# Another column order for the second token tile in every tail, and first products by arrival, in an encoder trunk

## The chip, the cores and the metric

The kernel runs on one core of one Trainium2 chip. The metric is the device time of one execution in microseconds, as the median of several executions. The kernel before took 935.35 us (median of three; 934.53 to 939.41). The profile shows one further execution.

## The reference

Two encoder layers of three sublayers each work on 256 tokens with 1024 features in fp32. So there are six stages: ffn, mLSTM, ffn, ffn, windowed attention, ffn. Each adds its result to a scaled x and normalises. Cut to what matters here:

```python
def swiglu(x, w_in, w_out):                       # w_in 1024 x 5632, w_out 2816 x 1024
    gu = x @ w_in
    g, u = gu[..., :D_FF], gu[..., D_FF:]
    return (jax.nn.silu(g) * u) @ w_out

for l in range(DEPTH):                            # DEPTH = 2
    x = layer_norm(ALPHA * x + 0.5 * swiglu(x, ffn_w_in[l, 0], ffn_w_out[l, 0]), ...)
    y = mlstm_mixer(x, ...) if l % 2 == 0 else window_attention(x, ...)
    x = layer_norm(ALPHA * x + y, ...)
    x = layer_norm(ALPHA * x + 0.5 * swiglu(x, ffn_w_in[l, 1], ffn_w_out[l, 1]), ...)
```

The mLSTM mixer projects x to q, k, v, output gate and 16 small gates (`gw` in the kernel), runs a chunked recurrence in both directions and projects back. Attention projects to q, k, v, attends within 128 tokens with a sink logit per head (`sink`), and projects back.

## The kernel before

**Products.** Every fp32 product is made of three single-pass products. Each operand is cut into a high part in TensorE's reduced fp32 form (ScalarE, `xT_hi`, `w_hi`, `h_hi`) and the rest (VectorE, `xT_lo`, `w_lo`, `h_lo`). `mm3` (L474) adds high by high, high by low and low by high into one PSUM bank. The stationary operand is a block of x or h transposed, 128 x 128; the moving one is 512 columns of a weight. The rows of the profile print them the other way: `pw<-w_hi,xT_lo` is the product of w's high and xT's low part. There are four PSUM banks named `pw` and four named `py`.

**Tokens and columns.** The 256 tokens are two tiles of 128, t = 0 and 1. A stage's output has 1024 columns, in two halves o = 0 and 1 of 512, so that y[t][o] takes the four `py` banks.

**Weights.** A piece is 128 x 1024 values. Its transfer (L102, issued by SyncE's queue) lands in one of four raw buffers (`w_raw`; six more, `s_raw`, hold pieces that are first added to one another, on VectorE or by an accumulating transfer that POOL issues, L265). `Weights.high` (L212) puts the split of ScalarE into the program, `Weights.low` (L236) that of VectorE. Both write into a ring of ten rooms. `Weights.take` (L288) hands pieces to the products; `Weights.done(upto, most)` (L297) says that the pieces before `upto` have had their last product, which opens rooms, and puts the splits of at most `most` further pieces into the program at this place. Within the ffn groups `Weights.fill` (L268) decides that instead, by a running model of the engines' times (`Paced`, L50). Transfers of raw pieces are issued, in the order of the plan, as the last reader of a raw buffer is done.

**Order.** The scheduler is switched off: every engine works through its instructions in the order in which the program wrote them, and waits at each until its operands are there. Because a helper records them, nearly all rows carry the line L136.

**The ffn.** One stage goes through its hidden columns in groups. `seven` (L727) takes a Strassen-like scheme with sums of x blocks (`S_hi`, `S_lo`) and of raw weights (`s_raw`). In the last group's `end4` VectorE multiplies by the activated gate (`e<-g,e`), and the block is transposed and split into `h_hi` and `h_lo` behind it.

**The tail.** `tail` (L554) ends a stage with the products of the last pieces: six in the ffn stages, eight in mLSTM, and in attention eight for tile 1. It runs over t, over o, and over the pieces. After each half `norm[t].half` adds the result to x (`x<-x,py`) and gathers its statistics; after both, `finish` (L533) makes rs with a power on POOL (L538) and normalises x in two passes, `x<-x,mv,ln_g` and `x<-x,rs,ln_b` (in two cuts each where `LC` says so). `emit_x(0)`, the transposes of tile 0's new x for the next stage, stands inside the last column pass of tile 1, at the piece `turn_at` = 4. The transposes of tile 1, `emit_x(1)`, are *pending*: the next stage runs them behind its first products, at the k-step that `PEND` gives. `TD` bounds how many splits stand behind the tail.

**The start.** While the first weights arrive, TensorE makes idle products on the identity (`warm`), transposes the first half of each token tile of x, and begins with the product of the first pieces.

**Small loads.** `small_loads` (L462) puts gate weights, gate biases and sinks on POOL's queue, with two negations; only mLSTM and attention use them.

Of the kernel before, what the change touches and what calls it, by code (L numbers as in the profile page):

```python
# [23 lines left out]
GROUPS = 3  # L24
# [7 lines left out]
FB = [1, 0, 1, 3, 2, 1, 0, 0, 1, 1, 0]  # L32
CT = [0, 1]
EX = [0, 1, 2, 2, 2, 2, 1, 2]
LC = [1, 0, 0, 0, 0, 1]
TD = [0, 3, 2, 0, 2, 1]
MP = [1, 0, 0, 0, 1, 0, 1, 1, 0, 0, 0, 0, 2, 2, 2]
PD = [8, 0, 7, 8, 5]
PEND = [6, 2, 6, 6, 6]


AHEAD = 300.0
# [276 lines left out]
def trunk_kernel(ctx: ExitStack, tc: tile.TileContext, x, ffn_w_in, ffn_w_out, ln_g, ln_b, ml_w_in, ml_gate_b,  # L319
                 ml_norm_g, ml_w_out, at_w_in, at_sink, at_w_out, out):  # L320
    nc = Paced(tc.nc)
# [152 lines left out]
    def mm3(o, l, r, start, stop, onto=False):  # L474
        nc.tensor.matmul(o, l[0], r[0], start=start, stop=False, skip_group_check=onto)
        nc.tensor.matmul(o, l[0], r[1], start=False, stop=False, skip_group_check=onto)
        nc.tensor.matmul(o, l[1], r[0], start=False, stop=stop, skip_group_check=onto)

    def pair(p, *idx):
        return p[0][idx], p[1][idx]  # L480
# [7 lines left out]
    A = slice(None)  # L488

    def tok(t):  # L490
        return slice(t * 128, (t + 1) * 128)

    def split_evac(dst, src, scale=None):
        if scale is None:
            nc.scalar.copy(dst[0], src)
            nc.vector.tensor_sub(dst[1], src, dst[0].bitcast(F32))
        else:
            nc.scalar.activation(dst[0], src, AF.Copy, scale=scale)
            nc.vector.scalar_tensor_tensor(dst[1], src, scale, dst[0].bitcast(F32), op0=OP.mult, op1=OP.subtract)

    def to_xT(t, src, bank, halves=range(2)):
        for h in halves:
            p = bank((128, 4, 128))
            for k in range(4):
                nc.tensor.transpose(p[:, k], src[:, (4 * h + k) * 128:(4 * h + k + 1) * 128], ident)
            split_evac(pair(xT, A, slice(4 * h, 4 * h + 4), tok(t)), p)

    def warm(n):

# [43 lines left out]

    def tail(y, h, todo, first, norm, last, turn_at, between=None):  # L554

        for t in range(2):
            for o in range(2):
                final = t == 1 and o == 1
                for n, (c, (i, w)) in enumerate(todo[t]):
                    if between is not None and t == 0 and o == 1 and n == turn_at:  # L560
                        between()
                    if final and n == turn_at:
                        emit_x(0, last)
                    mm3(y[t][o], h(c, t), pair(w, A, 0, slice(o * 512, o * 512 + 512)),
                        first and n == 0, n == len(todo[t]) - 1)
                    if final and n >= turn_at - 1:
                        W.done(i + 1, (0, 3, 0)[min(n - turn_at + 1, 2)])
                norm[t].half(o, y[t][o])
            norm[t].finish(t)
        W.done(most=TD[bound[0]])  # L570
        return lambda: emit_x(1, last)

    def emit_x(t, last):
        if not last:
            to_xT(t, xt[t], ybank)

    def ffn(l, i, n, pending, last):
        with ExitStack() as ph:
# [10 lines left out]
            start = pending is None  # L589
            if start:  # L590
                warm(14)
                to_xT(0, xt[0], ybank, (0,))
                W.split(1)
                warm(8)
                to_xT(1, xt[1], ybank, (0,))
                W.split(2)
            hs, pieces = [], []

            def tr(hB, t, h):
# [10 lines left out]
            def b_mm(ps, t, m, a):  # L610
                if 4 * m + a == len(pieces):
                    pieces.extend(W.take(1))
                for k in (2 * a, 2 * a + 1):
                    mm3(ps, pair(xT, A, k, tok(t)), pair(pieces[4 * m + a], A, k % 2), k == 0, k == 7)

            def b_silu(ps):
                sg = temp("sg")
# [38 lines left out]
            if start:  # L656
                sg = {}
                for m in range(2):
                    ps = [wbank(), wbank()]
                    for a in range(4):  # L660
                        if m == 0 and a == 1:
                            for t in range(2):
                                to_xT(t, xt[t], ybank, (1,))
                        for t in range(2):
                            b_mm(ps[t], t, m, a)
                            if m == 1 and a == 3:
                                b_mul(sg[t], ps[t])
                        early = {2: lambda: x_raw(0), 3: lambda: x_raw(1), 4: x_one, 5: x_two, 6: x_rest}
                        if 4 * m + a in early:
                            early[4 * m + a]()  # L670
                        W.done()
                    if m == 0:
                        W.open(pool, ends[bound[0]])
                        for t in range(2):
                            sg[t] = b_silu(ps[t])
            else:
                W.open(pool, ends[bound[0]])
                for t in range(2):
                    ps = [wbank(), wbank()]
                    for m in range(2):  # L680
                        for a in range(4):
                            if t == 0 and m == 1 and 2 * a == PEND[bound[0] - 1]:
                                pending()
                            b_mm(ps[m], t, m, a)
                            if t == 1:
                                W.done(W.used - 8 + 4 * m + a + 1)
                            if t == 1 and a % 2:
                                [[None, lambda: x_raw(0), None, lambda: x_raw(1)], [None, x_one, None, lambda: None]][m][a]()
                        if m == 0:
                            sg = b_silu(ps[0])  # L690
                            if t == 1:
                                tr(hB, 0, hs[0])
                    b_mul(sg, ps[1])
                x_two()
                W.done()
# [17 lines left out]
            def product(bank, x_of, first, then):  # L713

                for j in range(2):
                    w, = W.take(1)
                    for k in range(2):
                        mm3(bank, x_of(2 * j + k), pair(w, A, k), first and j == k == 0, j == k == 1, not first)
                then()
                W.done()  # L720
# [6 lines left out]
            def seven(full, unit_turn):  # L727

                of = lambda k0, t: (lambda k: pair(xT, A, k0 + k, tok(t)))
                sum_ = lambda name: (lambda k: pair(xs[name], A, k))  # L730
                v = {}
                hB = h_room(4)
                chunks(hB, 4)
                qa, qc = wbank(), wbank()

                def end1():
                    v["g0"] = copied(qa, "e1")

                def end2():
                    nc.vector.tensor_add(v["g0"], v["g0"], qc)  # L740

                def end5():
                    v["u1"] = copied(qb, "e5")

                def end6():
                    v["u0"] = copied(qa, "e2")
                    nc.scalar.activation(v["g0"], v["g0"], AF.Silu)

                def end3():
                    nc.vector.tensor_sub(v["u0"], qb, v["u0"])  # L750
                    nc.vector.tensor_mul(v["u0"], v["g0"], v["u0"])

                def end7():
                    nc.vector.tensor_sub(v["u1"], v["u1"], qa)

                def end4():
                    v["g1"] = temp("g1")
                    nc.scalar.activation(v["g1"], qa, AF.Silu)
                    nc.vector.tensor_mul(v["u1"], v["g1"], v["u1"])

                product(qa, of(0, 0), True, end1)
                unit_turn()
                product(qc, of(4, 0), True, end2)
                down(1)
                qb = wbank()
                product(qb, sum_("S1"), True, end5)
                product(qa, sum_("S2"), False, end6)
                down(1)
                product(qa, sum_("S3"), False, end7)
                product(qb, sum_("S4"), False, end3)  # L770
                if full:
                    down(1)
                    tr(hB, 0, v["u0"])
                product(qa, of(4, 1), False, end4 if full else lambda: (end4(), tr(hB, 0, v["u0"])))
                if full:
                    down(1)
                return lambda: tr(hB, 1, v["u1"])

            turn = None
            for g in range(GROUPS):  # L780
# [32 lines left out]
                if g == 0 and not start:  # L813
                    x_rest()
                turn = seven(g < GROUPS - 1, unit_turn)
                if start and g == 0:
                    small_loads()
            nc.filler = None
            gb = load_ln(lambda name: pool.tile([128, D], F32, name=name, tag="s_raw", bufs=S_RAW), l, n)
# [565 lines left out]
```

## Time and profile before

| | |
|---|---|
| median of three executions | 935.35 us |
| the profiled execution | 935.12 us |
| its span on the core | 933.4 us |
| busy: TensorE matmul / weight load | 920.0 / 769.0 us |
| busy: VectorE / ScalarE / POOL | 795.5 / 541.4 / 101.5 us |
| moved | 187.54 MB, mean 201 GB/s |

The span runs from the first to the last instruction of the profile, and the execution takes 1.7 us beyond it. In a row of the timeline the first number is the start in us from the span's begin, the second the time, then engine, line, operation, the tile written and those read, the shape, and in brackets how long the engine had been idle and what released it. `x2` and the like joins neighbours into one row. The profile models the end of a matmul: two that overlap in the rows are pipelined, and the spacing of their starts says more than their durations.

### The profile page before, as it was taken

What the parts mean: (1) busy time and instruction counts of PE and PEld (TensorE: products, weight loads), DVE (VectorE), ACT (ScalarE), POOL (GpSimd) and SP (SyncE); (2) the same over time, 40 slices, a digit from 0 to 9 for tenths busy, and PEclk for the clock granted to TensorE, in tenths of its full rate; (3) what the DMA queues carried; (4) which work ended last, traced back from release to release, by engine and by line L of the source; (5) the groups of instructions that cost most, each with busy time, mean ns of one, the idle gap of its engine ahead of it and who ended that gap; (6) DMA issues with size and microseconds to landing.
All of it is one profiled execution on the core that took longest, in us unless ns stands there. A gap on an engine that the chain in (4) does not pass through costs nothing.

```text
span 933.4 us, 12457 instructions
## 1 busy us (share of the span) xinstructions
PE 920.0 (99%) x4466; PEld 769.0 (82%) x4466; DVE 795.5 (85%) x967; ACT 541.4 (58%) x765; POOL 101.5 (11%) x181
## 2 busy tenths in 40 slices
PE   8999999999999999999999999999999999999996
PEld 7888888889988787888888888888898888888885
DVE  6899997786697889988878898978869798898975
ACT  5666756347563557575635566664568554757460
POOL 0030101011111000101010101010445300000100
PEclk9999999999999999999999999999999999999999
DMA  8979773646534858695559597836434376869531
GB/s 283 348 166 336 210 261 75 218 136 203 182 117 152 314 163 282 186 343 136 156 159 348 116 336 203 284 68 225 142 131 135 91 241 233 247 206 318 158 87 45
DMA packets 98461, 187.54 MB, mean 201 GB/s; under 512 B 6720, under 2 KB 37456, under 8 KB 98400
## 3 DMA queue, kind: packets, MB, share of 16 engines
q1 hardware_dynamic: 91072, 173.04, 54.1%
q0 software_dynamic: 6752, 12.66, 8.6%
q10 hardware_dynamic: 576, 1.05, 0.3%
q8 instruction: 35, 0.57, 0.3%
q14 instruction: 26, 0.21, 0.1%
HBM read 185.68 MB, written 1.05 MB: 200 GB/s over the span
## 4 chain that ended last, share of the span: by engine, by line
PE 83%; DVE 9%; DMA 2%; ACT 2%; issue 2%; SPq 1%; POOL 0%; DVEq 0%; ACTq 0%; POOLq 0%
PE pw L136 54%; PE py L136 29%; DVE w_lo L136 4%; DMA w_raw<-in_ffn_w_in_dram 1%; ACT w_hi L136 1%; DMA s_raw<-in_ffn_w_in_dram 1%; DVE x L136 1%; DVE h L136 1%; DVE s_raw L136 0%; DVE wt L136 0%; DVE h_lo L136 0%; SPq L102 0%; DVE a_lo L136 0%; ACT h L136 0%; DVE hst L136 0%
## 5 line engine op out<-in xcount | busy, mean ns | idle before, releaser
L136 DVE TENSOR_TENSOR w_lo<-w_raw,w_hi 128x1024 fp32r<-128x1024 f32 (+1 forms) x237 | 281.4, 1219 | 19.1 <-ACT w_hi L136 16.9
L136 ACT CAST w_hi<-w_raw 128x1024 fp32r<-128x1024 f32 (+1 forms) x237 | 240.9, 1049 | 73.2 <-DMA w_raw<-in_ffn_w_in_dram 19.2
L136 PE MATMUL pw<-w_hi,xT_hi 128*128 128x512 f32 x560 | 222.2, 397 | 0.0
L136 PE MATMUL pw<-w_hi,xT_lo 128*128 128x512 f32 x560 | 218.7, 390 | 0.0
L136 PE MATMUL pw<-w_lo,xT_hi 128*128 128x512 f32 x560 | 218.3, 390 | 0.2 <-DVE w_lo L136 0.2
L136 ACT CAST w_hi<-s_raw 128x1024 fp32r<-128x1024 f32 x144 | 148.4, 1052 | 97.7 <-DVE s_raw L136 62.0
L136 DVE TENSOR_TENSOR w_lo<-s_raw,w_hi 128x1024 fp32r<-128x1024 f32 x144 | 172.9, 1220 | 21.5 <-ACT w_hi L136 21.4
L136 PE MATMUL py<-w_hi,h_hi 128*128 128x512 f32 x352 | 138.0, 392 | 0.0
L136 PE MATMUL py<-w_hi,h_lo 128*128 128x512 f32 x352 | 137.3, 390 | 0.4 <-DVE h_lo L136 0.4
L136 PE MATMUL py<-w_lo,h_hi 128*128 128x512 f32 x352 | 137.1, 390 | 0.0
L136 PEld LDWEIGHTS pw<-w_hi,xT_lo 128*128 128x128 f32 x560 | 105.1, 188 | 22.6 <-DVE xT_lo L136 0.2
L136 PEld LDWEIGHTS pw<-w_lo,xT_hi 128*128 128x128 f32 x560 | 105.3, 188 | 21.2 <-DVE w_lo L136 0.7
L136 PEld LDWEIGHTS pw<-w_hi,xT_hi 128*128 128x128 f32 x560 | 105.2, 188 | 20.0
L136 DVE TENSOR_TENSOR s_raw<-s_raw 128x1024 f32<-128x1024 f32 x72 | 87.1, 1220 | 0.6
L265 POOL DMA_DIRECT2D s_raw<-in_ffn_w_in_dram x24 | 29.2, 1216 | 496.4 <-DVE w_lo L136 384.5
L136 PEld LDWEIGHTS py<-w_hi,h_lo 128*128 128x128 f32 x352 | 66.1, 188 | 15.3 <-DVE h_lo L136 1.6
L136 PEld LDWEIGHTS py<-w_lo,h_hi 128*128 128x128 f32 x352 | 66.1, 188 | 13.8 <-DVE w_lo L136 0.3
L136 PEld LDWEIGHTS py<-w_hi,h_hi 128*128 128x128 f32 x352 | 66.1, 188 | 13.2
L136 PE MATMUL pw<-w_hi,S_hi 128*128 128x512 f32 x192 | 74.8, 390 | 0.9 <-ACT e L136 0.9
L136 PE MATMUL pw<-w_hi,S_lo 128*128 128x512 f32 x192 | 74.7, 389 | 0.0
L136 PE MATMUL pw<-w_lo,S_hi 128*128 128x512 f32 x192 | 74.7, 389 | 0.0
L136 DVE TENSOR_TENSOR h_lo<-pw,h_hi 128x512 fp32r<-128x512 f32 x44 | 30.2, 688 | 23.9 <-ACT h_hi L136 23.7
(215 smaller groups left out, 1109.5 us busy)
## 6 DMA issues: line engine op xcount, KB each, us to landing
w_raw<-in_ffn_w_out_dram SPq DMA_DIRECT2D x88, 512.0 KB, 5.3
s_raw<-in_ffn_w_in_dram SPq DMA_DIRECT2D x72, 512.0 KB, 6.0
w_raw<-in_ffn_w_in_dram SPq DMA_DIRECT2D x56, 512.0 KB, 5.2
w_raw<-in_ffn_w_in_dram SPq DMA_DIRECT2D x96, 256.0 KB, 4.6
s_raw<-in_ffn_w_in_dram POOLq DMA_DIRECT2D x24, 512.0 KB, 6.1
w_raw<-in_ml_w_in_dram SPq DMA_DIRECT2D x24, 512.0 KB, 4.7
w_raw<-in_at_w_in_dram SPq DMA_DIRECT2D x12, 512.0 KB, 4.6
w_raw<-in_ml_w_out_dram SPq DMA_DIRECT2D x8, 512.0 KB, 3.4
```

What stands on the lines that cost most here:

```text
L136: r = f(out, *args, **kw)
L265: nc.gpsimd.dma_start(t.rearrange("p (k f) -> p k f", k=self.words[w]["k"]), v, accum_op=OP.add)
```

## The change

1. **The tail.** For tile 1 the order of the products changes. Half of the pieces (n < `half`) go to the second columns first, then all pieces to the first columns, then the rest to the second columns. Tile 0 is as before. A piece of the first half now has its last product during the pass over the first columns, and `done` is called for each piece from there on. The new table `RS` (eight numbers a stage) says how many splits each call puts into the program. `emit_x(0)` keeps its place among the matmuls. The residual of tile 1's first columns comes three pieces later in an ffn stage and four in mLSTM.
2. **Constants.** `LC[0]` 1 to 0: stage 0 normalises tile 1 in one pass. `TD[0]` 0 to 2. `PD[2]`, `PD[3]` (paces of the weight plan) each one lower. `PEND[1]` 2 to 4: the pending transposes of the ffn behind mLSTM stand one weight piece later.
3. **The start.** The copy of the high half of the first transposed tile goes from ScalarE to VectorE (`tensor_copy`). The first two pieces' products are ordered in `first_mm`; tile 1's transposes stand behind the first two products.
4. **`end4`.** The last group's transposes and split of tile 0 come ahead of the multiply `e<-g,e`.
5. **`small_loads`** is called in the last group of stage 0, not in the first.

```diff
-LC = [1, 0, 0, 0, 0, 1]
-TD = [0, 3, 2, 0, 2, 1]
+RS = [0, 0, 1, 0, 1, 0, 0, 0, 1, 0, 0, 3, 1, 0, 0, 0, 0, 0, 1, 0, 1, 1, 1, 0, 0, 0, 0, 0, 1, 2, 0, 0, 0, 0, 0, 0, 2, 1, 0, 1, 0, 0, 0, 1, 1, 3, 0, 0]
+LC = [0, 0, 0, 0, 0, 1]
+TD = [2, 3, 2, 0, 2, 1]
-PD = [8, 0, 7, 8, 5]
-PEND = [6, 2, 6, 6, 6]
+PD = [8, 0, 6, 7, 5]
+PEND = [6, 4, 6, 6, 6]
...
-        for t in range(2):
-            for o in range(2):
-                final = t == 1 and o == 1
-                for n, (c, (i, w)) in enumerate(todo[t]):
-                    if between is not None and t == 0 and o == 1 and n == turn_at:
-                        between()
-                    if final and n == turn_at:
-                        emit_x(0, last)
-                    mm3(y[t][o], h(c, t), pair(w, A, 0, slice(o * 512, o * 512 + 512)),
-                        first and n == 0, n == len(todo[t]) - 1)
-                    if final and n >= turn_at - 1:
-                        W.done(i + 1, (0, 3, 0)[min(n - turn_at + 1, 2)])
-                norm[t].half(o, y[t][o])
-            norm[t].finish(t)
+        def one(t, o, n):
+            c, (i, w) = todo[t][n]
+            mm3(y[t][o], h(c, t), pair(w, A, 0, slice(o * 512, o * 512 + 512)), first and n == 0, n == len(todo[t]) - 1)
+
+        for o in range(2):
+            for n in range(len(todo[0])):
+                if between is not None and o == 1 and n == turn_at:
+                    between()
+                one(0, o, n)
+            norm[0].half(o, y[0][o])
+        norm[0].finish(0)
+        full = len(todo[1])
+        half = full // 2
+        order = [(1, n) for n in range(half)] + [(0, n) for n in range(full)] + [(1, n) for n in range(half, full)]
+        more = iter(RS[8 * bound[0]:8 * bound[0] + 8])
+        for j, (o, n) in enumerate(order):
+            if j == full + turn_at:
+                emit_x(0, last)
+            one(1, o, n)
+            if j >= half and (n < half) == (o == 0):
+                W.done(todo[1][n][1][0] + 1, next(more))
+            if n == full - 1:
+                norm[1].half(o, y[1][o])
+        norm[1].finish(1)
         W.done(most=TD[bound[0]])
...
-                to_xT(0, xt[0], ybank, (0,))
+                to_xT(0, xt[0], ybank, (0,), nc.vector.tensor_copy)
                 W.split(1)
                 warm(8)
-                to_xT(1, xt[1], ybank, (0,))
-                W.split(2)
...
+            def first_mm(ps, a):
+
+                def mm(t, i, j):
+                    for k in (2 * a, 2 * a + 1):
+                        nc.tensor.matmul(ps[t], xT[i][:, k, tok(t)], pieces[a][j][:, k % 2], start=i == j == k == 0,
+                                         stop=False)
+
+                if a == 1:
+                    for t in range(2):
+                        to_xT(t, xt[t], ybank, (1,))
+                pieces.extend(W.take(1))
+                mm(0, 0, 0)
+                if a == 0:
+                    to_xT(1, xt[1], ybank, (0,))
+                    W.split(2)
+                mm(0, 1, 0)
+                if a == 0:
+                    mm(0, 0, 1)
+                mm(1, 0, 0)
+                if a == 0:
+                    mm(1, 0, 1)
+                mm(1, 1, 0)
+                if a == 1:
+                    mm(0, 0, 1)
+                    mm(1, 0, 1)
...
                 def end4():
                     v["g1"] = temp("g1")
                     nc.scalar.activation(v["g1"], qa, AF.Silu)
+                    if not full:
+                        tr(hB, 0, v["u0"])
                     nc.vector.tensor_mul(v["u1"], v["g1"], v["u1"])
...
-                product(qa, of(4, 1), False, end4 if full else lambda: (end4(), tr(hB, 0, v["u0"])))
+                product(qa, of(4, 1), False, end4)
...
-                if start and g == 0:
+                if start and g == GROUPS - 1:
                     small_loads()
```

More of the change, by code (lines that the diff above doesn't have):

```diff
@@ L491, in tok, with split_evac @@
         return slice(t * 128, (t + 1) * 128)
-    def split_evac(dst, src, scale=None):
+    def split_evac(dst, src, scale=None, high=None):
         if scale is None:
-            nc.scalar.copy(dst[0], src)
+            (high or nc.scalar.copy)(dst[0], src)
             nc.vector.tensor_sub(dst[1], src, dst[0].bitcast(F32))
@@ L499, in split_evac, with to_xT @@
             nc.vector.scalar_tensor_tensor(dst[1], src, scale, dst[0].bitcast(F32), op0=OP.mult, op1=OP.subtract)
-    def to_xT(t, src, bank, halves=range(2)):
+    def to_xT(t, src, bank, halves=range(2), high=None):
         for h in halves:
@@ L505, in to_xT @@
                 nc.tensor.transpose(p[:, k], src[:, (4 * h + k) * 128:(4 * h + k + 1) * 128], ident)
-            split_evac(pair(xT, A, slice(4 * h, 4 * h + 4), tok(t)), p)
+            split_evac(pair(xT, A, slice(4 * h, 4 * h + 4), tok(t)), p, high=high)
     def warm(n):
@@ L660, in ffn @@
                     for a in range(4):
-                        if m == 0 and a == 1:
-                            for t in range(2):
-                                to_xT(t, xt[t], ybank, (1,))
+                        if m == 0 and a < 2:
+                            first_mm(ps, a)
                         for t in range(2):
-                            b_mm(ps[t], t, m, a)
+                            if m or a > 1:
+                                b_mm(ps[t], t, m, a)
                             if m == 1 and a == 3:
```

## The prediction

> **What bounds the kernel now.** I read first the page's shares, then the granted clock and the chain, then a table of stretches for TensorE alone, and last the timeline around each gap.
>
> ```profile
> span 933.4 us, 12457 instructions
> ...
> PE 920.0 (99%) x4466; PEld 769.0 (82%) x4466; DVE 795.5 (85%) x967; ACT 541.4 (58%) x765; POOL 101.5 (11%) x181
> ...
> 513.34 5.44 PE py L136 x24
> ...
> 0.00:12.00 12.00, 9.63 (x52) 1.00 0.82 294
> ...
> 236.00:278.00 42.00, 41.54 (x240) 1.00 0.39 137
> 278.00:311.00 33.00, 31.84 (x151) 1.00 0.52 166
> 320.00:360.00 40.00, 39.14 (x177) 1.00 0.69 214
> 442.00:490.00 48.00, 47.78 (x223) 1.00 0.50 154
> 622.00:668.00 46.00, 45.77 (x215) 1.00 0.48 156
> ```
>
> In the stretches the columns are length, PE's busy time (instructions), granted clock, DMA share and GB/s. PE is busy 920.0 of 933.4 us, and the clock is 1.00 in each stretch shown. Twenty-four products of the chain start in 5.44 us: 0.227 us apart. The change removes no matmul, so all it can win is PE's idle time, 13.4 us in all. Taking length less busy time, the stretches it touches hold 2.37 (0 to 12), 1.16 (the seam behind mLSTM), 0.86 (first groups of the ffn behind it), 0.22 and 0.23 (two ffn seams). That is under 5 us, 0.5% of the time, which is also about what a measurement of this kernel can tell from no change.
>
> The profiled execution took 935.12 us, 1.7 beyond its span and 0.23 below the median of 935.35.
>
> **The start.** Three edits go together: VectorE instead of ScalarE copies the high half of the first transposed tile, products are issued in the order in which their operands arrive, and the second tile's transposes go behind two products.
>
> ```profile
> 5.71 0.58 ACT L136 CAST xT_hi<-py 128x512 fp32r<-128x512 f32 x1 [1.49 <-PE py L136]
> ...
> 6.33 0.69 DVE L136 TENSOR_TENSOR xT_lo<-py,xT_hi 128x512 fp32r<-128x512 f32 x1 [4.94 <-ACT xT_hi L136]
> ...
> 6.93 0.66 PE L136 MATMUL py<-ident,x 128*128 128x128 f32 x4 [0.38 <-DMA x<-in_x_dram]
> ...
> 11.10 0.47 PE L136 MATMUL pw<-w_hi,xT_hi 128*128 128x512 f32 x1
> ...
> 11.79 0.50 PE L136 MATMUL pw<-w_lo,xT_hi 128*128 128x512 f32 x1 [0.22 <-DVE w_lo L136]
> ...
> 13.00 1.23 DVE L136 TENSOR_TENSOR w_lo<-w_raw,w_hi 128x1024 fp32r<-128x1024 f32 x1
> ...
> 13.76 0.39 PE L136 MATMUL pw<-w_hi,xT_hi 128*128 128x512 f32 x1
> ```
>
> PE waits 0.38 us for the second x tile at 6.93, and the second product of weight piece 1 starts 0.69 behind the first, 0.46 over the spacing. With the w_lo products last in that piece, eight others (1.8 us) stand ahead of the first of them, so the 0.46 goes. The 0.38 goes if the two moved products are ready; the copy now costs a pass of VectorE. No row has a plain VectorE copy out of PSUM: its bounds are free (the ScalarE pass that it replaces leaves ScalarE earlier for w_hi) and one more 0.69, 0.11 over ScalarE's 0.58. I take 0.69, since the nearest row is a VectorE pass from the same bank. Together the cap is 0.84, but piece 2 is late next. The row at 13.76 is the tenth of piece 1's twelve products, so the w_lo product of piece 2 stands at 13.76 + 4 x 0.227 = 14.67 before; its w_lo ends at 14.23, behind two xT_lo passes which the change leaves ahead of it. So at most 0.44 survives. I take 0.4, bounds 0 and 0.75 (if VectorE's queue comes forward too).
>
> [...]
>
> **The tails.** Each ends a stage: the second token tile formerly did its 1st columns, then its 2nd; now half of the 2nd, all of the 1st, the rest of the 2nd. The matmuls are the same and the first tile's transposes keep their place among them. Rooms of the weight ring come free earlier, and a table says how many splits (ScalarE w_hi, VectorE w_lo) are issued at each. What moves on VectorE: in stage 0 one w_lo stands before the residual of the 1st columns and one, not three, before that of the 2nd; in mLSTM four before and one between, not three between; in the third stage one before and two between. In the fourth stage and in attention the order on VectorE stays.
>
> ```profile
> 185.72 1.29 DVE L136 TENSOR_TENSOR xT_lo<-py,xT_hi 128x512 fp32r<-128x512 f32 x2 [1.74 <-ACT xT_hi L136]
> ...
> 289.86 1.28 DVE L136 SCALAR_TENSOR_TENSOR x<-x,rs,ln_b 128x1024 f32<-128x1024 f32 x1 [0.45 <-POOL rs L538]
> 291.25 0.69 DVE L136 SCALAR_TENSOR_TENSOR x<-x,py 128x512 f32<-128x512 f32 x1
> ...
> 295.04 1.29 DVE L136 TENSOR_TENSOR xT_lo<-py,xT_hi 128x512 fp32r<-128x512 f32 x2 [2.36 <-ACT xT_hi L136]
> 296.47 3.50 DVE L136 TENSOR_TENSOR w_lo<-w_raw,w_hi 128x1024 fp32r<-128x1024 f32 x3
> ...
> 297.86 0.39 PE L136 MATMUL pw<-w_hi,xT_lo 128*128 128x512 f32 x1
> ...
> 477.65 0.69 DVE L136 TENSOR_TENSOR xT_lo<-py,xT_hi 128x512 fp32r<-128x512 f32 x1 [1.75 <-ACT xT_hi L136]
> ```
>
> A w_lo in a row takes 3.50/3 = 1.17 us. In stages 0 and 2 one more fits into the idle 1.74 and 1.75 ahead of xT_lo: hidden, 0.6 to spare. In mLSTM four do not fit quite: from 291.14 they end at 295.81, the residual (PE is done with it at 291.25 + 4 pieces x 3 x 0.227 = 293.97) and its statistics, as long again, at 297.2, and the first xT_lo at 297.9, wanted at 297.86. I charge 0.1 there, and between 0 and 0.3.
>
> ```profile
> 303.97 1.28 DVE L136 SCALAR_TENSOR_TENSOR x<-x,rs,ln_b 128x1024 f32<-128x1024 f32 x1
> 303.98 0.39 PE L136 MATMUL pw<-w_hi,xT_lo 128*128 128x512 f32 x1
> ...
> 305.31 1.09 PE L136 MATMUL py<-ident,x 128*128 128x128 f32 x8 [0.94 <-DVE x L136]
> ```
>
> The 305.31 transposes are the largest seam gap: 1.33 after the product before, 1.11 over the spacing. They wait for x times rs, which ends at 305.25; nothing brings that forward (its residual at the tail's end is set by PE). But the other constant, PEND[1] from 2 to 4, puts them one piece later, six matmuls or 1.36 us: wanted at 304.21 + 1.36 = 305.57, after 305.25. So 1.11 goes, less the 0.1 above: 1.0, bounds 0.6 and 1.1.
>
> ```profile
> 198.51 0.28 PE L136 MATMUL pw<-xT_hi,gw_hi 128*128 128x256 f32 x1
> ...
> 198.88 0.38 PE L136 MATMUL pw<-xT_lo,gw_hi 128*128 128x256 f32 x1
> ...
> 355.06 0.39 PE L136 MATMUL py<-w_hi,h_lo 128*128 128x512 f32 x1
> ...
> 356.31 0.50 PE L136 MATMUL pw<-w_hi,S_hi 128*128 128x512 f32 x1 [0.86 <-ACT e L136]
> ```
>
> At 198.51 two 256-column products start 0.37 apart; two halves of 0.227 would be 0.12, so 0.25 is lost to xT_lo. Normalising in one pass (LC[0] to 0) and fewer w_lo behind it bring it forward: 0.2, bounds 0 and 0.26. At 355.06 the gap is 1.25, 1.02 over the spacing, with ScalarE and VectorE behind on the S sums and the raw pieces that they need. The splits behind x times rs at 303.97 end 1.17 us earlier, one more being done in the tail, and with them the raw rooms and their loads. How much of that lead lives 45 us later no row shows: bounds 0 and 1.02, I take half, 0.5.
>
> **End of the last group.** In four ffn stages VectorE now makes h_lo ahead of the multiply e.
>
> ```profile
> 461.30 0.68 DVE L136 TENSOR_TENSOR e<-g,e 128x512 f32<-128x512 f32 x1
> ...
> 461.90 0.68 DVE L136 TENSOR_TENSOR h_lo<-pw,h_hi 128x512 fp32r<-128x512 f32 x1
> 462.03 0.39 PE L136 MATMUL py<-w_lo,h_hi 128*128 128x512 f32 x1
> ...
> 462.64 0.50 PE L136 MATMUL py<-w_hi,h_lo 128*128 128x512 f32 x1 [0.22 <-DVE h_lo L136]
> ...
> 641.60 0.50 PE L136 MATMUL py<-w_hi,h_lo 128*128 128x512 f32 x1 [0.23 <-DVE h_lo L136]
> ```
>
> The product that needs h_lo starts 0.61 behind the one before, 0.38 too late, here and at 641.60; moved up by a 0.60 pass it is in time. The multiply's reader is six matmuls behind. Twice 0.38: 0.76, bounds 0 and 0.78.
>
> **Small loads** go from the first to the last group of stage 0, on POOL's queue behind six accumulating loads.
>
> ```profile
> 72.05 0.33 POOL L471 TENSOR_SCALAR neg_sink<-sink 128x16 f32<-128x16 f32 x1 [5.59 <-DMA sink<-in_at_sink_dram]
> ...
> 155.00:160.00 5.00, 5.00 (x24) 4.14 (x23) 2.94 (x4) 4.58 (x7) 0.00 (x0) 1.00 0.01 3
> ...
> 179.80 1.53 POOL L538 TENSOR_TENSOR rs<-rs,mhalf 128x1 f32<-128x1 f32 x1 [34.66 <-DVE rs L136]
> ```
>
> POOL was held 5.59 us by the sink; held as long near 150 us it is free long before its next work at 179.80, in a stretch where the DMA share is 0.01. Nothing; without that cover rs, and the mLSTM seam, would be late by up to 5.59.
>
> **Sum.** 0.4 + 0.2 + 1.0 + 0.5 + 0.76 = 2.9 us: 935.1 becomes 932.3 profiled, and with the 0.23 a median of 932.5 (-0.3%). All lower bounds give 934.7 as median, all upper ones 931.4.
>
> **Rivals.** (A) The gaps move. PE starts early but VectorE, 85% busy, and the raw loads give it the next gap: start and 355 lose their 0.9, 303.98 keeps 0.4 of its gap: 935.35 - 1.6 = 933.8. For it: piece 2's w_lo is already the next wait. Against: h_lo and the pending transposes have nothing behind them.
>
> (B) Slower. A piece is split earlier than its raw data has landed; w_hi then stands in ScalarE's queue ahead of the first tile's xT_hi, or w_lo in VectorE's ahead of the residual, and PE waits for xT.
>
> ```profile
> w_raw<-in_ffn_w_in_dram SPq DMA_DIRECT2D x56, 512.0 KB, 5.2
> ...
> 287.00:295.00 8.00, 8.00 (x41) 6.74 (x40) 4.97 (x8) 0.58 (x2) 1.53 (x1) 1.00 0.03 9
> ```
>
> A load lands 5.2 us after its issue; on average half would be waited out, 2.6. Of it 0.6 is spare in stages 0 and 2, nothing in mLSTM: 2.0 + 2.0 + 2.6 = 6.6, less the start and h_lo (1.2): 940.7. It passes 0.5% from a wait of 2.4 per seam. Against: from 287 to 295 the DMA share is 0.03, so the four raw buffers there are full before the early splits; the fifth is not.
>
> (C) Faster: every gap goes fully (0.75 + 0.26 + 1.1 + 1.02 + 0.78 = 3.9) and the lead also takes the 0.46 of the stretch 236 to 278 and half of the start's other 1.6: 930.2. Against: there the waits are inside mLSTM's own chain.
>
> (D) PE is not the bound and VectorE is: nothing won, 935.3. Against: VectorE idles 15%, and each PE gap above ends by one named wait. [...]
>
> **How the numbers follow.** Forecast 0.50, A 0.18, B 0.13, C 0.11, D 0.08. Only C ends faster by over 0.5% (below 930.7): 0.11; only B slower (above 940.0): 0.13; within: 0.76. The range leaves out half of C and most of B: 930.3 to 937; the forecast's own is 931.4 to 934.7.
>
> **What would show it.** Right: no gap over 0.3 at the second product of piece 1, at both h_lo products, at the transposes near 304; span 930.5. Wrong: xT_hi or xT_lo(0) waited for by PE behind a tail, a new gap at piece 2 over 0.5, the 355 gap unchanged, or POOL's rs late near 180.

## The result and the profile after

The changed kernel takes 932.38 us (median of 8; 931.33 to 933.91), the kernel before on the same chip 935.69 (8 runs). The ratio is 0.9966, 95% interval 0.9956 to 0.9975: 3.3 us less. The forecast was 932.5, and the measured time lies inside the stated range of 930.3 to 937. The profiled execution of after took 933.63 us, on the long side of the eight, with a span of 931.9; its trace shows 1.5 us less span than that of before, and why it is not 3.3 is told below.

The first lines of the page of after, and the table of stretches for TensorE (length, busy time and instructions, granted clock, DMA share, GB/s):

```profile
span 931.9 us, 12472 instructions
...
PE 920.1 (99%) x4466; PEld 769.3 (83%) x4466; DVE 796.8 (86%) x966; ACT 542.6 (58%) x764; POOL 102.2 (11%) x181
...
0.00:12.00 12.00, 10.27 (x54) 1.00 0.82 292
...
278.00:311.00 33.00, 32.75 (x156) 1.00 0.68 217
320.00:360.00 40.00, 40.00 (x182) 1.00 0.67 205
442.00:490.00 48.00, 48.00 (x226) 1.00 0.55 171
622.00:668.00 46.00, 46.00 (x216) 1.00 0.50 160
```

TensorE's work is the same, and its idle time is gone from the stretches that the prediction named: 1.16 became 0.25 behind mLSTM, 0.86 became 0 in the ffn behind it, 0.22 and 0.23 became 0 at the two ffn seams. The start has 1.73 in place of 2.37. The timeline of after at those places, for TensorE and VectorE, and at two places that had no gap before:

```profile
306.19 1.03 PE L137 MATMUL py<-ident,x 128*128 128x128 f32 x8
...
354.74 0.39 PE L137 MATMUL pw<-w_hi,S_hi 128*128 128x512 f32 x1
...
459.75 0.68 DVE L137 TENSOR_TENSOR h_lo<-pw,h_hi 128x512 fp32r<-128x512 f32 x1
460.35 0.68 DVE L137 TENSOR_TENSOR e<-g,e 128x512 f32<-128x512 f32 x1
...
460.69 0.39 PE L137 MATMUL py<-w_hi,h_lo 128*128 128x512 f32 x1
...
63.09 0.50 PE L137 MATMUL py<-w_lo,h_hi 128*128 128x512 f32 x1 [0.62 <-DVE w_lo L137]
...
803.35 0.50 PE L137 MATMUL pw<-w_hi,S_hi 128*128 128x512 f32 x1 [0.44 <-ACT e L137]
```

The transposes, the S product and the product that needs h_lo (460.69) carry no bracket any more: TensorE waited for nothing there. The last two rows are new waits, at 63 and 803 us, where the orders of TensorE, VectorE and ScalarE are those of before. The question for the experiments is whether they are its price, and which part of the change removed which gap.

### The profile page after: what moved, and what is told of

The parts are those of the page before. It is cut to its first block, busy times and chain, and to the rows that moved or that the text cites. A ratio compares the mean times of both kernels' runs of the same rounds, so it can differ in the third digit from the quotient of the medians.

```text
span 931.9 us, 12472 instructions
## 1 busy us (share of the span) xinstructions
PE 920.1 (99%) x4466; PEld 769.3 (83%) x4466; DVE 796.8 (86%) x966; ACT 542.6 (58%) x764; POOL 102.2 (11%) x181
## 3 DMA queue, kind: packets, MB, share of 16 engines
q10 hardware_dynamic: 576, 1.05, 0.3%
HBM read 185.68 MB, written 1.05 MB: 200 GB/s over the span
## 4 chain that ended last, share of the span: by engine, by line
PE 82%; DVE 9%; DMA 3%; ACT 3%; issue 2%; SPq 1%; DVEq 0%; ACTq 0%
PE pw L137 52%; PE py L137 30%; DVE w_lo L137 4%; ACT w_hi L137 1%; DMA s_raw<-in_ffn_w_in_dram 1%; DMA w_raw<-in_ffn_w_out_dram 1%; DVE s_raw L137 1%; SPq L103 1%; DVE h L137 1%; DVE x L137 1%; DMA w_raw<-in_ffn_w_in_dram 0%; DMA x<-in_x_dram 0%; DVE e L137 0%; ACT xT_hi L137 0%; DVE wt L137 0%
```

## The experiments

In the following table each matmul of the trace is counted through (4466 in every kernel), and its start is compared with that of the same count in before: minus is earlier. The first two columns are that difference at counts which before reaches at 60 and 74 us, the next six are how it changes over a stretch, and the last is where it ends. One profiled execution each.

```
kernel        at 60  at 74 | 198-216 294-325 351-366 454-472 519-563 629-652 |  end
after         -0.36  +0.70 |  -0.37   -1.20   -1.00   -0.51   +0.38   -0.51  | -1.48
same_again    -0.49  +1.23 |  -0.37   -1.20   -1.00   -0.49   +0.17   -0.48  | -1.67
a_pend2       -0.68  -0.19 |  -0.36   -1.11   -0.99   -0.46   +0.18   -0.46  | -2.90
a_oldstart    -0.16  +0.37 |  -0.36   -1.20   -1.00   -0.48   +0.76   -0.46  | -2.39
a_oldend      -0.45  -0.20 |  -0.37   -1.21   -1.00   +0.02   +0.18   +0.02  | -2.29
a_smallearly  +1.31  +1.43 |  -0.37   -1.20   -1.00   -0.51   +0.73   -0.48  | -1.35
a_three       +0.25  +0.23 |  -0.36   -1.20   -1.00   -0.48   +0.19   -0.51  | -1.78
combined      -0.73  +0.07 |  -0.36   -1.20   -1.00   -0.46   +0.41   -0.51  | -2.97
b_tail        +1.21  +1.23 |  -0.36   -1.16   -1.04   +0.02   +0.16   +0.01  | -1.03
b_order       -0.16  +0.07 |  +0.00   +0.02   -0.74   +0.04   +0.13   -0.01  | -0.39
b_pend4       -0.37  -0.35 |  +0.02   -0.39   +0.47   +0.02   +0.00   +0.03  | -0.12
b_start       +0.05  +0.07 |  -0.01   -0.03   +0.44   +0.00   +0.00   +0.03  | +0.85
b_smalllate   -0.16  -0.17 |  +0.00   +0.00   -0.65   +0.02   +0.02   +0.03  | +0.21
```

Names that begin with a are the changed kernel with one part undone or altered, those with b the kernel before with one part added.

**The changed kernel again** (no edit).

> The changed kernel unedited, once more. Theory: the gaps that went (products of piece 1, transposes near 304, the S product near 355, both h_lo products near 462 and 641) are gone in every execution, since they hang on the order of the instructions; the three that are new in its first profile (0.78 us near 62, 0.33 near 541, 0.60 near 803) hang on when transfers land and shift or vanish from one execution to the next: time 932.4, span 930.0 to 931.0. Rival: the new gaps are the price of the change and come back at the same places with 0.3 to 0.8 us each: span again 931.9.

Measured: 933.17 us, ratio 0.9973 (0.9962 to 0.9983), span 931.7. The gap at 803 was gone and that near 541 down to 0.11; the one at 62 to 63 came back, larger (0.92 and 0.76 over the spacing on two products). So the theory held for two of three, and the rival for the wait near 62. The span, too, is nearer the rival's 931.9 than the theory's 930 to 931. The row of ScalarE that starts the wait near 62, in before and in this execution, is the split of one piece near 39 us:

```profile
38.79 1.06 ACT L136 CAST w_hi<-w_raw 128x1024 fp32r<-128x1024 f32 x1 [0.86 <-DMA w_raw<-in_ffn_w_out_dram]
```

```profile
40.46 1.05 ACT L137 CAST w_hi<-w_raw 128x1024 fp32r<-128x1024 f32 x1 [3.09 <-DMA w_raw<-in_ffn_w_out_dram]
```

It waits 0.86 us for its transfer in one, 3.09 in the other. From there VectorE works with hardly a pause up to 62 us (in this execution it is busy 9.53 of the ten from 50 to 60), so what is late at 40 is late at 62: in after, w_lo of that piece starts at 40.97, 1.09 behind that of before, and the one at 61.81 is still 0.68 behind. TensorE, if it comes early to 62, waits there.

**PEND[1] alone.**

```diff
-PEND = [6, 2, 6, 6, 6]
+PEND = [6, 4, 6, 6, 6]
```

> The kernel before with one constant of the change, PEND[1] 4 in place of 2, so the pending transposes behind mLSTM stand six matmuls later. Theory: the gap of 1.11 us at 304 goes, and the S product near 355, whose chain of raw loads, splits and sums has not moved, takes it over: 1.02 grows to about 2.1, and the time stays 935.5. Rival (the gap is simply removed): 355 keeps its 1.02 and the time is 934.5.

Measured: 935.0 us, ratio 0.9992 (0.9982 to 1.0001). The transposes wait for nothing, and other products wait in their place (timeline of that kernel, TensorE):

```profile
305.26 1.03 PE L136 MATMUL py<-ident,x 128*128 128x128 f32 x8
...
309.26 0.50 PE L136 MATMUL pw<-w_hi,xT_hi 128*128 128x512 f32 x1 [0.24 <-ACT xT_hi L136]
...
355.13 0.50 PE L136 MATMUL pw<-w_hi,S_hi 128*128 128x512 f32 x1 [0.34 <-ACT e L136]
...
364.41 0.63 PE L136 MATMUL pw<-ident,e 128*128 128x128 f32 x4 [0.81 <-DVE e L136]
```

At 294 us this kernel is 0.31 ahead of before, at 308, behind the transposes, 1.49: 1.2 gained. Of it 0.8 is lost at 309 to 312, where products wait for the split of the moved transposes. Near 355 and 364 this kernel loses 0.47 more than before does at 355. The theory named the S product alone, which lost 0.5, not 2.1. The first loss shows that by itself this constant moves a wait; the second is not surely its own, since `b_start` (below) loses 0.44 in the same stretch without it.

**The change without PEND[1].**

```diff
-PEND = [6, 4, 6, 6, 6]
+PEND = [6, 2, 6, 6, 6]
```

> The changed kernel with PEND[1] back at 2. Theory: the gap at 304 is back with 1.0 to 1.2 us, since x times rs still ends near 305.2, and the S product near 355 has no gap; the time is 933.4. Rival (the early splits of the tail alone feed the S product and the pending transposes do nothing for the time): 932.4.

Measured: 932.28 us, ratio 0.9964 (0.9951 to 0.9977), and no gap near 304. My theory fell, and the rival's time came: the transposes at their old place do not wait.

**The tail alone** (function `tail` with RS, LC, TD and PD of the change; PEND[1] stays 2).

```diff
-LC = [1, 0, 0, 0, 0, 1]
-TD = [0, 3, 2, 0, 2, 1]
+RS = [0, 0, 1, 0, 1, 0, 0, 0, 1, 0, 0, 3, 1, 0, 0, 0, 0, 0, 1, 0, 1, 1, 1, 0, 0, 0, 0, 0, 1, 2, 0, 0, 0, 0, 0, 0, 2, 1, 0, 1, 0, 0, 0, 1, 1, 3, 0, 0]
+LC = [0, 0, 0, 0, 0, 1]
+TD = [2, 3, 2, 0, 2, 1]
...
-PD = [8, 0, 7, 8, 5]
+PD = [8, 0, 6, 7, 5]
```

> The kernel before with the tail of the change alone (the new order of tile 1, RS, LC, TD, PD), PEND, start, h_lo and small loads as before. Theory: the gap at 304 stays (1.1), the S product near 355 loses its gap (1.0) and the gate product near 198.5 loses its 0.26: 934.2. Rival (the S product's lead comes from elsewhere): 355 keeps its 1.02, the time stays 935.3.

Measured: 933.47 us, ratio 0.9973 (0.9964 to 0.9982); all three gaps went, that at 304 too, which the theory had kept. The timeline of this kernel shows why (VectorE, and TensorE's transposes of the two tiles):

```profile
294.65 1.03 PE L137 MATMUL py<-ident,x 128*128 128x128 f32 x8
...
291.37 4.62 DVE L137 TENSOR_TENSOR w_lo<-w_raw,w_hi 128x1024 fp32r<-128x1024 f32 x4
295.92 0.68 DVE L137 SCALAR_TENSOR_TENSOR x<-x,py 128x512 f32<-128x512 f32 x1
297.24 1.27 DVE L137 TENSOR_TENSOR xT_lo<-py,xT_hi 128x512 fp32r<-128x512 f32 x2
298.43 1.22 DVE L137 TENSOR_TENSOR w_lo<-w_raw,w_hi 128x1024 fp32r<-128x1024 f32 x1
299.56 0.68 DVE L137 SCALAR_TENSOR_TENSOR x<-x,py 128x512 f32<-128x512 f32 x1
...
303.64 1.28 DVE L137 SCALAR_TENSOR_TENSOR x<-x,rs,ln_b 128x1024 f32<-128x1024 f32 x1
...
305.08 1.03 PE L137 MATMUL py<-ident,x 128*128 128x128 f32 x8
```

```profile
293.78 1.03 PE L136 MATMUL py<-ident,x 128*128 128x128 f32 x8
...
297.18 0.39 PE L136 MATMUL py<-w_hi,xT_lo 128*128 128x512 f32 x1
...
299.88 0.68 DVE L136 SCALAR_TENSOR_TENSOR x<-x,py 128x512 f32<-128x512 f32 x1
```

The second fence is before. Its row at 297.18 is the tail's last product: TensorE is done at 297.57, and the residual of the second columns, which reads the sum, starts 2.31 us later. So VectorE's queue holds it up, not TensorE. It starts 6.10 us behind the transposes of tile 0 (293.78 to 299.88), directly behind three w_lo; with the tail it starts 4.91 behind them (294.65 to 299.56), directly behind one. So x times rs ends 10.27 behind them, not 11.47, and TensorE wants it at 10.43.

**The new order without early splits.** The base is the kernel before with the new order of products; the table makes the splits where they were, and VectorE's order is that of before to the instruction.

```diff
+RS = [0, 0, 0, 0, 3, 0, 0, 0] * 6
```

> The kernel before with the new order of tile 1's products alone: the table makes no early splits but the old ones (three at the fifth piece of the last pass), LC, TD, PD, PEND, start, h_lo and small loads are as before, and VectorE's order is that of before to the instruction. Theory (the gain comes from splits done early, not from the order as such): the gaps near 304 (1.1) and 355 (1.0) stay, the time is 935.5. Rival (the order itself frees VectorE or raw buffers): one of the two goes and the time is 934.5 or less.

Measured: 935.31 us, ratio 0.9995 (0.9986 to 1.0004). The gap at 304 stays: 

```profile
305.42 0.77 PE L137 MATMUL py<-ident,x 128*128 128x128 f32 x5 [0.96 <-DVE x L137]
```

Near 355 only 0.26 stood, not 1.0, but without any effect on the time that can be told, and the kernel with the small loads alone (below) had 0.38 there and that with the start alone 1.47: this gap differs between executions as long as the tail does not feed it. The order of products by itself gains nothing that can be measured; what it does is to free rooms for early splits.

**One split too many.** Three early splits in place of one in the third stage.

```diff
-0, 0, 1, 0, 1, 1, 1, 0,   (third stage's eight of RS)
+0, 0, 3, 0, 0, 0, 0, 0,
```

The two splits that the changed kernel makes between the two residuals fall away in return, so that three stand in the tail either way.

> The changed kernel with three splits, in place of one, ahead of the residual of tile 1's first columns in the third stage (RS for that stage 0,0,3,0,...); nothing else. Theory (VectorE's queue ahead of the first xT_lo is the limit of early splits): three w_lo of 1.17 each end at 475.9, residual and statistics at 477.2, the first xT_lo at 477.9, which TensorE wants at 477.05: a new gap of 0.8 to 0.9 us there, 0.8 longer in all. Rival (half a microsecond of spare time more, or the lead gives it back behind): no gap over 0.3 near 477, the time is that of the changed kernel.

Measured: 933.49 us, ratio 0.9975 (0.9963 to 0.9986). VectorE and TensorE of that kernel:

```profile
471.99 3.49 DVE L137 TENSOR_TENSOR w_lo<-w_raw,w_hi 128x1024 fp32r<-128x1024 f32 x3
...
476.73 1.27 DVE L137 TENSOR_TENSOR xT_lo<-py,xT_hi 128x512 fp32r<-128x512 f32 x2
...
476.40 0.39 PE L137 MATMUL pw<-w_lo,xT_hi 128*128 128x512 f32 x1
477.45 0.50 PE L137 MATMUL pw<-w_hi,xT_lo 128*128 128x512 f32 x1 [0.66 <-DVE xT_lo L137]
477.79 0.39 PE L137 MATMUL pw<-w_hi,xT_hi 128*128 128x512 f32 x1
478.02 0.40 PE L137 MATMUL pw<-w_lo,xT_hi 128*128 128x512 f32 x1
```

The product that needs xT_lo starts 1.05 behind the one before, 0.82 over the spacing, as expected, and the kernel loses 0.97 between 472 and 519 us, where no other kernel loses over 0.05. By 629 nothing of it is given back. So VectorE's queue ahead of the first xT_lo is what limits early splits. Three are too many by 0.82 us; two, one w_lo of 1.17 fewer, would fit by an estimate from this trace (not run).

**The old start in the changed kernel** (transposes of tile 1 and the splits ahead of the first products, products piece by piece, copy on ScalarE).

```diff
-                to_xT(0, xt[0], ybank, (0,), nc.vector.tensor_copy)
+                to_xT(0, xt[0], ybank, (0,))
                 W.split(1)
                 warm(8)
+                to_xT(1, xt[1], ybank, (0,))
+                W.split(2)
...
-                        if m == 0 and a < 2:
-                            first_mm(ps, a)
+                        if m == 0 and a == 1:
+                            for t in range(2):
+                                to_xT(t, xt[t], ybank, (1,))
                         for t in range(2):
-                            if m or a > 1:
+                            if True:
                                 b_mm(ps[t], t, m, a)
```

> The changed kernel with the start of before (high half by ScalarE, second tile's transposes ahead of the first products, products piece by piece). Theory: TensorE is 0.4 to 0.8 us later at 14 us, and this costs nothing in the end, because a raw piece that lands near 39 us sets VectorE's and ScalarE's pace up to 62, where the changed kernel then waits 0.6 to 1.7; here no gap over 0.3 stands near 62 and the time is 932.4 to 932.8. Rival (the waits near 62 have nothing to do with the start): a gap of 0.6 or more stands near 62 here too, and the time is 933.2 or more.

Measured: 932.78 us, ratio 0.9966 (0.9954 to 0.9978): the time of the changed kernel, as the theory said. But 0.64 stood near 62 here too, as the rival said, so the wait there is not the new start's alone.

**The start alone in the kernel before** (the same edit the other way).

> The kernel before with the start of the change alone. Theory: it is 0.4 to 0.8 us ahead at 14 us, waits near 62 for w_lo as long or longer, and takes 935.6, no gain. Rival (the gain stays): no gap near 62, 935.2.

Measured: 935.69 us, ratio 1.0001 (0.9991 to 1.0010): no gain. The expected lead and the wait at 62 were both absent: this execution was 0.21 ahead at 14 us and 0.05 behind at 60.

**The old order of h_lo in the changed kernel.**

```diff
-                    if not full:
-                        tr(hB, 0, v["u0"])
...
-                product(qa, of(4, 1), False, end4)
+                product(qa, of(4, 1), False, end4 if full else lambda: (end4(), tr(hB, 0, v["u0"])))
```

> The changed kernel with h_lo behind the multiply again at the end of the last group. Theory: 0.40 over the spacing at the h_lo product comes back in the stages that had it, near 460 and 639, and nothing else changes: 0.8 to 1.0 us longer, 933.4. Rival (the time is given back behind, at the seam): the time is the changed kernel's, 932.5.

Measured: 933.12 us, ratio 0.9975 (0.9964 to 0.9986). Both waits are back:

```profile
460.20 0.50 PE L137 MATMUL py<-w_hi,h_lo 128*128 128x512 f32 x1 [0.23 <-DVE h_lo L137]
...
639.34 0.50 PE L137 MATMUL py<-w_hi,h_lo 128*128 128x512 f32 x1 [0.23 <-DVE h_lo L137]
```

In the table every kernel with the new order gains 0.46 to 0.51 at each of the two seams, and every one with the old order 0.04 or less. The medians alone (933.12 against 932.38 and 933.17) would not have told it.

**Small loads in the first group again, in the changed kernel.**

```diff
-                if start and g == GROUPS - 1:
+                if start and g == 0:
```

> The changed kernel with the small loads in the first group again. Theory: they neither help nor hurt; the wait near 62 is as with the change (0.6 to 1.7), since it comes from a raw piece landing near 39, and the time is 932.5 to 933.2. Rival (moving them is what loosens or tightens the loads near 62): the gap there goes, or grows by 1 us or more, and the time moves with it.

Measured: 931.72 us, ratio 0.9960 (0.9946 to 0.9973), no gap near 62; but TensorE was 1.31 late at 60 in this execution (1.08 already at 14) and had nothing to wait for. Neither theory is borne out by it; the next run and the last one decide.

**Small loads late, in the kernel before** (the same edit the other way).

> The kernel before with the small loads alone moved to the last group. Theory (moving them, 40 us ahead of where they stood, has to do with the late landing of raw pieces): SyncE takes 6.9 to 7.3 us for its eight 256 KB issues from 16.5 on, against 6.3 before, and a gap of 0.3 to 1 us stands near 62; the time is 935.9 to 936.4. Rival (the landings of the first 40 us vary from execution to execution, whatever the small loads do): 6.3 us, no gap near 62, 935.7.

Measured: 935.44 us, ratio 0.9998 (0.9988 to 1.0007), no gap near 62. SyncE's eight issues take 6.52 us here; in `b_order`, with the small loads at their old place, they took 7.20 (SyncE's queue in both):

```profile
16.33 6.52 SPq L100 DMA_DIRECT2D w_raw<-in_ffn_w_in_dram  x8
```

```profile
16.28 7.20 SPq L101 DMA_DIRECT2D w_raw<-in_ffn_w_in_dram  x8
```

The theory that the small loads slow the first landings fell. What these issues show is something else. Over all fourteen traces they take 6.97 to 7.27 us in the seven kernels that lose 0.23 us or more between 60 and 74, and 6.17 to 6.52 in the seven that lose 0.12 or less. Old and new start, early and late small loads stand on both sides. So the wait near 62 goes with how the early transfers run in an execution, not with a part of the change.

**Tail, start and h_lo, without the two other parts** (small loads in the first group, PEND[1] 2).

> The changed kernel with the two parts undone that the runs show no gain for: small loads in the first group, PEND[1] 2. Theory: the tail and the h_lo order carry the whole gain; no gap over 0.3 near 62 and 304; time 931.5 to 932.3. Rival (the pending transposes need the later place when VectorE is slower in the tail): a gap of 0.3 or more near 304, 932.5 or more.

Measured: 932.71 us, ratio 0.9964 (0.9951 to 0.9976), no wait near 304. But the wait near 62 is there, with the small loads early:

```profile
62.47 0.50 PE L137 MATMUL py<-w_lo,h_hi 128*128 128x512 f32 x1 [0.61 <-DVE w_lo L137]
```

So that wait needs neither the late small loads nor the late transposes. The theory's time, 931.5 to 932.3, was missed: the version is not faster than the changed kernel by more than the intervals, and no gain or loss of these two parts can be told from the medians.

## Why the prediction was right

The sum was right, 2.9 us against 3.3, with the likeliest case (only idle time of TensorE can be won, and most named gaps go). That it came so close is in part luck. The start gave nothing that can be told, where 0.4 was forecast, and a loss of 0.35 near 541 was not foreseen; the gate product, the transposes, the S product and h_lo together gave 1.0 more than forecast. Term by term, with the column means of the table for the kernels that have the part:

**Start, 0.4: nothing that can be told.** The 0.46 ahead of the w_lo product went as forecast, but the prediction looked only one piece ahead for what is late next. What is late next is a transfer: the traces of before and of the changed kernel's second execution have waits of 0.86 and 3.09 us for the piece that is split near 39 us, and the four kernels that are 0.4 or more ahead at 60 lose 0.25 to 1.7 by 74. In the mean of the table the eight kernels with the new start are 0.14 ahead at 60 and 0.42 behind at 74, the others (before among them) 0.06 and 0.19 behind. `b_start` measured 1.0001, but its interval (0.9991 to 1.0010) and the spread at 60 us, about 2 us, would not show a gain as small as 0.4. Rival A named this mechanism, at the wrong place. The copy on VectorE took what I had charged, 0.69:

```profile
5.81 0.69 DVE L137 CAST xT_hi<-py 128x512 fp32r<-128x512 f32 x1 [4.42 <-PE py L137]
```

It is as long as the two-operand pass out of PSUM that the prediction shows at 6.33 in before, 0.69.

**Gate product at 198, 0.2: 0.36.** Right in kind. It goes with the tail in all nine kernels that have it, and not with the order of products alone. Whether RS, LC[0] or TD[0] does it was not separated.

**Transposes at 304, 1.0: 1.2, and the step was wrong.** The step said that x times rs comes no earlier, because its residual is set by TensorE, and that PEND[1] removes the gap. The row at 296.47, three w_lo that end as the residual starts, was quoted in the prediction and read for its price only: TensorE was done at 297.57, and VectorE's own queue set the residual. The tail takes two of the three out of it, and that is the gain; `a_pend2` and `b_pend4` show that the constant adds none. The 0.1 charged for an xT_lo that comes late in mLSTM did not occur either: no product of `b_tail` waits between 294 and 309.

**S product at 355, 0.5: about 0.9.** The tail removes it wholly: -0.99 to -1.04 in nine of nine. The kernels without it, before included, average -0.1, from -0.74 to +0.47. So the prediction's halving was too careful, and the row of before was one draw of a gap that varies. That raw loads come forward with the tail shows in the first sum piece that ScalarE splits, in before (quoted first) and after:

```profile
321.26 1.05 ACT L136 CAST w_hi<-s_raw 128x1024 fp32r<-128x1024 f32 x1 [2.04 <-DMA s_raw<-in_ffn_w_in_dram]
```

```profile
317.48 1.05 ACT L137 CAST w_hi<-s_raw 128x1024 fp32r<-128x1024 f32 x1
```

3.8 us earlier, and without a wait. How this reaches 355 shows on VectorE, in before and after. The S product waits for e, which ScalarE copies behind two splits; these wait for a sum that VectorE makes at 352.53 in before and 349.98 in after:

```profile
346.79 0.69 DVE L136 TENSOR_TENSOR h_lo<-pw,h_hi 128x512 fp32r<-128x512 f32 x1 [0.28 <-ACT h_hi L136]
347.39 1.22 DVE L136 TENSOR_TENSOR s_raw<-s_raw 128x1024 f32<-128x1024 f32 x1
...
352.53 1.22 DVE L136 TENSOR_TENSOR s_raw<-s_raw 128x1024 f32<-128x1024 f32 x1
```

```profile
345.37 0.69 DVE L137 TENSOR_TENSOR h_lo<-pw,h_hi 128x512 fp32r<-128x512 f32 x1 [0.28 <-ACT h_hi L137]
...
349.98 1.22 DVE L137 TENSOR_TENSOR s_raw<-s_raw 128x1024 f32<-128x1024 f32 x1
```

Before has another sum in between, at 347.39, and the last one starts 5.74 behind h_lo; after has made it further up and starts 4.61 behind. All nine kernels with the tail have the short queue; `b_order`, `b_start` and `b_smalllate` have that of before. So here, too, the tail takes a pass out of VectorE's queue, and its 1.13 us is about the 1.02 of the gap. The early order alone did not do this. PD cannot have done it: the kernel reads it only in mLSTM and attention, and of its two changed entries only PD[3], in attention (PD[2] is never read). mLSTM's LC and TD are the same as well, which leaves RS, unless stage 0's LC[0] and TD[0] still act here; that was not run.

**h_lo, 0.76: 0.97.** Right, and mis-sized by the same 0.1 a place as the other gaps (below).

**Small loads, nothing: perhaps a loss of 0.3.** As forecast, POOL's rs near 180 was not late: at 180.49 in after it waits for VectorE, not for these loads. But six of the seven kernels that load them late (all but `a_oldstart`) lose 0.25 to 0.31 us between 257 and 294 us, inside mLSTM, and the seven that load them early 0.02 at most. How the small loads could do this is open, and the medians do not resolve it.

**What the sum left out.** Near 541 TensorE waits for a multiply of VectorE that makes e (at 541.86 in after, 0.17 idle). The kernels with the tail lose 0.16 to 0.76 there, 0.35 in the mean, the others 0.13 or less. The loss does not follow their lead at 519 us (0.18 with a lead of 2.8, 0.73 with 1.55). It goes with VectorE's order: two w_lo stand ahead of that multiply in all nine (538.03 and 539.17 in after), one in the five others (540.53 in before), as the running model of the ffn groups places the splits otherwise. That is a new gap as in rival A, for a ninth of the gain. With it the terms come to 0.36 + 1.2 + 0.9 + 0.97 - 0.35 = 3.1, and with mLSTM's 0.3 to 2.8, against 3.3 measured (2.3 to 4.1 by its interval). A change of up to 0.7 near 803 differs between executions of like kernels; its cause stays open. The profiled execution of after had the waits at 63, 541 and 803 together, and so shows 1.5.

**Rival B** (slower, by splits whose data has not landed) did not occur: in mLSTM four w_lo follow one another in 4.62 us, without a wait. Its other half, a queue too long ahead of xT_lo, is real two splits further, as `a_three` shows. Rival D is out: VectorE was given no less work, and the time fell.

## What to carry to other kernels

Where one engine is busy 99%, list its gaps with what ended each, and ask of each who sets the releaser: at 304 and 355 the releaser's place in VectorE's in-order queue set it (the residual 2.31 us behind its last product, the sum 1.13 later for another ahead of it). At 304, moving two of the splits that stood directly ahead of it into idle time further up gave more than moving its reader (1.16 us in `b_tail`, 0.39 in `b_pend4`). The gap removed at the start, in a stretch that goes as its transfers land, was no gain that can be told (`b_start`, 1.0001); look at the next wait for a transfer, not only at the next instruction. With changes of tenths, one profile is one draw: what stands at the same place in nine kernels and is absent in the others tells more than the medians.

## What the runs showed of the hardware that was not expected

In these traces a wait of TensorE costs more than itself. Behind the product that waited in `a_three`, the next starts 0.34 us later (477.45 to 477.79) and the one after that 0.23 (477.79 to 478.02): some 0.11 us beyond the usual 0.227. The h_lo gaps of 0.38 gave back 0.46 to 0.51, the 1.11 at the transposes 1.11 to 1.21, and the 0.26 at the gate product 0.36.

The start varied by two microseconds between executions of nearly the same program: TensorE at 14 us stood between 1.15 ahead of before (`combined`) and 1.08 behind (`a_smallearly`), and both have the same start.
